# How a split SiLU-and-multiply kernel opens and closes its stores: six first transfers with small packets, 4-row chunks in tile 0, a last tile in two stores

## The chip, the cores and the metric

The kernel runs on one core of a Trainium2 chip. The metric is the device time of one execution in microseconds (us), as the median of several runs. Times inside an execution are taken from its profile and count from the start of the profiled span.

## The reference

```python
batch, seq, dim = (32, 512, 2048)          # x: float32
half_dim = x.shape[-1] // 2
x1, x2 = x[..., :half_dim], x[..., half_dim:]
return (x1 * (1 / (1 + np.exp(-x1))) * x2).astype(np.float32)
```

134.2 MB are read and 67.1 MB written; the arithmetic is one SiLU and one multiply per output element.

## The kernel before

The 16,384 rows are worked off in 16 tiles. A tile has 128 partitions with K = 8 rows each, so a load is 8 MiB in runs of 64 KiB per partition and a store 4 MiB in runs of 32 KiB. There are two input buffers and two output buffers. SiLU runs on ScalarE (ACT) and writes the output tile, the multiply on VectorE (DVE). Loads are issued on the sync queue, stores on the queue of ScalarE.

```python
K = 8
KC_EDGE = 2
OPENING = [                                   # first store: partitions, rows
    (slice(0, None, 4), slice(0, 2)),         # 32 partitions, 8 KiB runs
    (slice(0, None, 4), slice(2, None)),      # 32 partitions, 24 KiB
    (slice(2, None, 4), slice(None)),         # 32 partitions, 32 KiB
    (slice(1, None, 2), slice(None)),         # 64 partitions, 32 KiB
]
in_pool = ctx.enter_context(tc.tile_pool(name="in_pool", bufs=2))
out_pool = ctx.enter_context(tc.tile_pool(name="out_pool", bufs=2))
# ... (cut: the views, load(), silu() on ACT, mul() on DVE)
load(0)
load(1)
for i in range(n_tiles):
    # ... (cut)
    if i < n_tiles - 1:
        kc = KC_EDGE if i == 0 else K
        for c in range(0, K, kc):
            silu(ot, xt, c, c + kc)
            mul(ot, xt, c, c + kc)
        for ps, ks in OPENING if i == 0 else [(slice(None), slice(None))]:
            nc.scalar.dma_start(out=ov[ps, ks], in_=ot[ps, ks])
        if i + 2 < n_tiles:
            load(i + 2)
        continue
    # ... (cut: the last tile, four chunks and four stores of 2 rows)
```

The comments beside OPENING are ours.

## Time and profile before

| | before |
|---|---|
| time, median of 4 runs | 470.53 us (470.48 to 470.60) |
| span of the profiled run | 468.5 us |
| DVE, ACT busy | 30%, 24% |
| load queue and store queue, share of 16 DMA engines | 66.4% and 33.2% |

The lines themselves, and how they are read, stand in the prediction.

### The profile page before, as it was taken

The numbers are of one execution on the slowest core, as the hardware profiler recorded it, in microseconds if no ns is written. First come the engines' busy times: TensorE is split into PE (matmuls) and PEld (weight loads), VectorE is DVE, ScalarE is ACT, GpSimd is POOL, SyncE is SP. The second block draws the span as 40 slices with busy tenths as digits, with TensorE's granted clock in tenths as the row PEclk, the third lists the DMA queues.
The fourth block names the chain that finished last, engine by engine and source line by source line (L and its number), as shares of the span: only waits on it lengthen the run. The fifth ranks groups of instructions, "written<-read, shape, count | busy, mean of one in ns | idle before, by whom it ended". The sixth has DMA issues, their size and how long they took to land.

```text
span 468.5 us, 188 instructions
## 1 busy us (share of the span) xinstructions
DVE 139.5 (30%) x22; ACT 114.3 (24%) x23; POOL 0.2 (0%) x4
## 2 busy tenths in 40 slices
DVE  0070613407033070430704207052060510606151
ACT  1142306041060500505005050140601406023060
POOL 0000000000000000000000000000000000000000
DMA  9999999999999999999999999999999999999988
GB/s 431 392 453 380 448 425 425 492 403 403 448 476 420 403 448 425 470 403 428 422 492 403 403 448 487 408 403 448 425 470 403 425 425 492 403 403 448 481 371 357
DMA packets 5121, 201.34 MB, mean 430 GB/s; under 512 B 608, under 2 KB 608, under 8 KB 608
## 3 DMA queue, kind: packets, MB, share of 16 engines
q1 hardware_dynamic: 2304, 134.22, 66.4%
q10 hardware_dynamic: 2816, 67.11, 33.2%
q14 instruction: 1, 0.01, 0.0%
HBM read 134.22 MB, written 67.11 MB: 430 GB/s over the span
## 4 chain that ended last, share of the span: by engine, by line
DMA 72%; DVE 14%; ACT 11%; DVEq 0%; issue 0%; ACTq 0%
DMA xt<-in_x_dram 72%; DVE ot L91 14%; ACT ot L84 11%; DVEq L148 0%; ACTq L84 0%
## 5 line engine op out<-in xcount | busy, mean ns | idle before, releaser
L91 DVE TENSOR_TENSOR ot<-ot,xt 128x8192 f32<-128x8192 f32 (+1 forms) x22 | 139.5, 6362 | 319.6 <-ACT ot L84 319.6
L84 ACT ACTIVATE ot<-xt 128x8192 f32<-128x8192 f32 (+1 forms) x22 | 113.0, 5163 | 340.5 <-DMA xt<-in_x_dram 340.5
L84 ACT ACT_TABLE_LOAD x1 | 1.3, 1283 | 0.8 <-PEq L137 0.8
L137 POOL MEMSET const-bfloat16-1.0<- 128x1 bf16 x1 | 0.1, 101 | 0.0
L137 POOL MEMSET const-uint8-127<- 128x1 uint8 x1 | 0.1, 101 | 0.0
L137 POOL MEMSET const-float32-0.0<- 128x1 f32 x1 | 0.1, 98 | 0.2 <-issue 0.2
L137 POOL MEMSET const-float32-1.0<- 128x1 f32 x1 | 0.1, 98 | 0.0
## 6 DMA issues: line engine op xcount, KB each, us to landing
out_dram<-ot ACTq DMA_DIRECT2D x14, 4096.0 KB, 42.0
out_dram<-ot ACTq DMA_DIRECT2D x5, 1024.0 KB, 8.2
out_dram<-ot ACTq DMA_DIRECT2D x1, 2048.0 KB, 37.0
out_dram<-ot ACTq DMA_DIRECT2D x1, 768.0 KB, 11.7
xt<-in_x_dram SPq DMA_DIRECT2D x16, 42.1
out_dram<-ot ACTq DMA_DIRECT2D x1, 256.0 KB, 10.9
```

What stands on the lines that cost most here:

```text
L84: nc.scalar.activation(out=ot[:, c:ce, :], in_=xt[:, c:ce, :half], func=mybir.ActivationFunctionType.Silu,)
L91: nc.vector.tensor_mul(out=ot[:, c:ce, :], in0=ot[:, c:ce, :], in1=xt[:, c:ce, half:],)
L137: nc = _bacc.Bacc("TRN2", target_bir_lowering=False, num_devices=1)
```

## The change

The diff suggests this intent: smaller packets at the head of the first store, so that the store takes less from the loads behind which it starts; fewer and larger instructions in tile 0; and fewer, larger stores at the end.

```diff
-    KC_EDGE = 2
+    CHUNKS_FIRST = [4, 4]
+    CHUNKS_LAST = [2, 2, 4]
+    KS = 4
     OPENING = [
         (slice(0, None, 4), slice(0, 2)),
-        (slice(0, None, 4), slice(2, None)),
-        (slice(2, None, 4), slice(None)),
+        (slice(0, None, 4), slice(2, 4)),
+        (slice(0, None, 4), slice(4, None)),
+        (slice(2, None, 4), slice(0, 4)),
+        (slice(2, None, 4), slice(4, None)),
         (slice(1, None, 2), slice(None)),
     ]
 ... (cut: the loop over the chunks of tile 0 now takes CHUNKS_FIRST)
-        cuts = list(range(0, K, KC_EDGE))
 ... (cut: four chunks, each stored two steps later)
+        for kc in CHUNKS_LAST:
+            silu(ot, xt, c, c + kc)
+            if issued is None and c >= KS:
+                issued = slice(0, KS)
+                nc.scalar.dma_start(out=ov[:, issued], in_=ot[:, issued])
+            mul(ot, xt, c, c + kc)
+            c += kc
+        nc.scalar.dma_start(out=ov[:, KS:], in_=ot[:, KS:])
```

More of the change, by code (lines that the diff above doesn't have):

```diff
@@ L103 @@
         if i < n_tiles - 1:
-            kc = KC_EDGE if i == 0 else K
-            for c in range(0, K, kc):
+            c = 0
+            chunks = CHUNKS_FIRST if i == 0 else [K]
+            for kc in chunks:
                 silu(ot, xt, c, c + kc)
                 mul(ot, xt, c, c + kc)
+                c += kc
             for ps, ks in OPENING if i == 0 else [(slice(None), slice(None))]:
@@ L113 @@
             continue
-        cuts = list(range(0, K, KC_EDGE))
-        for n, c in enumerate(cuts + [None, None]):
-            if c is not None:
-                silu(ot, xt, c, c + KC_EDGE)
-                mul(ot, xt, c, c + KC_EDGE)
-            if n >= 2:
-                b = cuts[n - 2]
-                nc.scalar.dma_start(out=ov[:, b:b + KC_EDGE, :], in_=ot[:, b:b + KC_EDGE, :])
+        issued = None
+        c = 0
+        for kc in CHUNKS_LAST:
[4 more added lines that the diff above has]
+            mul(ot, xt, c, c + kc)
+            c += kc
+        nc.scalar.dma_start(out=ov[:, KS:], in_=ot[:, KS:])
 _INS = ['x']
```

## The prediction

> **What bounds the kernel now.** I read the page first: busy shares, the slices, the chain.
>
> ```profile
> span 468.5 us, 188 instructions
> DVE 139.5 (30%) x22; ACT 114.3 (24%) x23; POOL 0.2 (0%) x4
> ...
> DMA  9999999999999999999999999999999999999988
> ...
> q1 hardware_dynamic: 2304, 134.22, 66.4%
> q10 hardware_dynamic: 2816, 67.11, 33.2%
> ...
> DMA 72%; DVE 14%; ACT 11%; DVEq 0%; issue 0%; ACTq 0%
> ```
>
> Both compute engines are idle most of the time. The load queue (q1) and the store queue (q10) together fill 99.6% of the 16 DMA engines. The compute in the chain only separates one load from the next; it lies beside other transfers. The single-packet records of the trace say the same more sharply: from the first load packet, 1.0 us into the span, to the last store packet, which ends at 467.1, no engine pauses visibly. So the kernel moves 201.33 MB with no hole, and only about 1.0 us at the start and 1.4 at the end are not transfer. **There is nearly nothing left to win; the question is whether the change opens a hole.**
>
> The durations come from the groups kept apart by shape:
>
> ```profile
> L91 DVE TENSOR_TENSOR ot<-ot,xt 128x8192 f32<-128x8192 f32 x14 | 121.7, 8692 | 280.6 <-ACT ot L84 280.6
> L84 ACT ACTIVATE ot<-xt 128x8192 f32<-128x8192 f32 x14 | 98.4, 7029 | 298.7 <-DMA xt<-in_x_dram 298.7
> L91 DVE TENSOR_TENSOR ot<-ot,xt 128x2048 f32<-128x2048 f32 x8 | 17.8, 2286 | 39.0 <-ACT ot L84 39.0
> L84 ACT ACTIVATE ot<-xt 128x2048 f32<-128x2048 f32 x8 | 14.6, 1897 | 41.8 <-DMA xt<-in_x_dram 41.8
> ```
>
> A whole tile needs 7.03 + 8.69, with 0.03 between them: 15.75 us from data to store. A 4-row chunk (4096 elements per partition), on the straight line through the two sizes, needs 3.6 us of SiLU and 4.4 of multiply.
>
> Then the timeline of the start:
>
> ```profile
> 21.88 5.51 ACT L84 ACTIVATE ot<-xt 128x2048 f32<-128x2048 f32 x3 [19.83 <-DMA xt<-in_x_dram]
> 23.82 8.90 DVE L91 TENSOR_TENSOR ot<-ot,xt 128x2048 f32<-128x2048 f32 x4 [23.82 <-ACT ot L84]
> 26.15 0.55 ACTq L110 DMA_DIRECT2D out_dram<-ot  x1
> 27.30 1.89 ACT L84 ACTIVATE ot<-xt 128x2048 f32<-128x2048 f32 x1
> 32.75 1.78 ACTq L110 DMA_DIRECT2D out_dram<-ot  x3
> 44.34 7.03 ACT L84 ACTIVATE ot<-xt 128x8192 f32<-128x8192 f32 x1 [15.15 <-DMA xt<-in_x_dram]
> ```
>
> Tile 0 lands at 21.9, its first store goes out at 26.15, the other three from 32.75, and load 1 lands at 44.3.
>
> **The turns.** In the packet records each engine alternates: one packet of the store queue, one of the load queue. A load packet is 64 KiB (2.418 us), a store packet 8 KiB (0.309), 24 KiB (0.912) or 32 KiB (1.213); 16 KiB is then some 0.61. Every transfer ends with a 4-byte packet (9 ns), and that takes a turn too. A full load is 8 + 1 turns, a full store 8 + 1 turns, so in steady state they go in step: 8 x (2.418 + 1.213) = 29.05 us per tile.
>
> The first store sets the phase. Today it has (2+1) + (2+1) + (2+1) + (4+1) = 14 turns. Its first packet goes out with packet 5 of load 1, so there are 5 turns of load 1 left (four packets and its end) and 9 of load 2: also 14. In the records the ends of store 0 and of load 2 do fall in the same turn. This tie matters because there are only two output buffers: SiLU of tile 2 needs load 2 **and** the end of store 0.
>
> **What the Trainium skill says.** "DMA: Bandwidth & Descriptors", section "Queues, rings and completion order": an engine goes round-robin between the queues it has work for, a packet at a time. The trace agrees; but here the switch comes after every single run of 64 or 32 KiB. The same page, "Why a DMA increments its semaphore by 16 and not by 1": the number of engines follows from the outer dimension, and each used engine posts its end. The trace agrees: the transfers of 32 partitions appear as 16 packets twice over, and each transfer leaves 16 packets of 4 bytes. "Latency and other measured facts" there gives about 600 ns to the first byte; the trace's first load took 1.0 us from its issue to its first packet.
>
> **The change part by part.**
>
> Tile 0 in chunks of 4 rows: SiLU 21.88 + 3.6, multiply + 4.4, so the first two stores go out at 29.95 instead of 26.15; the second multiply ends at 34.4 instead of 32.7, then four stores and load 2. Load 2 queues behind load 1, so that delay costs nothing. No engine is idle either: load 1 still has packets. Direct cost 0.
>
> When does the first store packet get a turn? Today it was issued at 26.15, missed the boundary at 28.1 and was taken at 30.7. So it lets pass the packet that runs when it arrives and one more. Issued at 29.95, it falls in load packet 5 (30.5 to 32.9, counting 2.418 a packet from 20.83) or just before, lets packet 6 pass, and is taken at **35.35**, with packet 7.
>
> Six transfers: turns (2+1) + (2+1) + (2+1) + (2+1) + (2+1) + (4+1) = **20 instead of 14**. Of these 3 go with load 1 (packets 7, 8, end), 9 with load 2, and 8 with the eight packets of load 3. In time:
> - load 1 ends at 35.35 + 2 x (0.31 + 2.42) = 40.8, about 3 us earlier than now;
> - load 2 ends at 40.8 + 8 x 2.418 + 2 x 0.31 + 4 x 0.61 = 63.2 (now near 70.1);
> - store 0 ends at 63.2 + 7 x 2.418 + 2 x 0.61 + 4 x 1.213 = 86.2.
>
> To that come 0.45 for the last engine, 0.37 from its end packet to the start of the waiting SiLU (both as in the records of now), and about 1 us, because load packets near the first stores took up to 2.7 to 3.1 us: tile 2 starts at **88.0**, not at 71.27, although its data lie there since about 64.
>
> Tile 2 then takes 15.75 us, so load 4 and store 2 are issued at 103.75 and begin at 104.8. Until then the engines have only loads 0 to 3 and stores 0 and 1, and these bytes were through by 99.2 in the kernel before (SiLU of tile 3 started at 100.05, less the 0.82). **So a hole of 5 to 6 us opens once.** Afterwards load 4 and store 2 start together with 9 turns each and are again in step: end at 104.8 + 29.05 = 133.8, SiLU of tile 4 at 134.6 where the timeline has 129.17 now. Shift **+5.4 us**, and no later stage gives it back, as no stage has spare DMA time.
>
> The last tile: its 32 packets of 8 KiB per engine become 16 of 16 KiB; (32 x 0.309) - (16 x 0.61) = 0.1 us less. Its first store goes out 6.5 us after the data (1.9 + 2.3 + 2.3) instead of 4.3. The store before it keeps the engines busy for 8 x 1.213 = 9.7 us from the end of the last load, 8.9 from the start of SiLU, so 2.4 us are left for the way from issue to first packet, where load 0 took 1.0. Expected cost 0. The second half, at 11.8 us, comes before the first half is through (8.9 + 4.9).
>
> Sum: 470.49 + 5.4 - 0.1 = 475.8.
>
> **The rivals.**
> - *Nothing opens.* If the engines hold enough work to bridge tile 2, only the order of bytes moves: 470.4. For it: 99.6% busy. Against it: at the end of store 0 there is left one load packet and store 1, 2.4 + 9.7 = 12.1 us, against 15.75 + 1.0 + 0.8 needed.
> - *One boundary earlier.* The first packet goes with packet 6: store 0 ends 2.4 us earlier and the hole is 3 us: 473.4. One single observation fixes that latency (over 2.0, under 4.6 us after issue; 3.0 would do), so I give this 30%. A boundary later would make it 478, 5%.
> - *The tail goes dry.* If a store needs over 2.4 us to its first packet, 0 to 2 us are added.
> - *A gain from the earlier loads.* Loads 1 and 2 land 3 and 7 us earlier, but the bytes are the same and the engines were never idle: worth nothing.
>
> **Range and chances.** Weights 0.6 for 475.8, 0.3 for 473.4, the rest for 470.4 and 478, and some tenths for the tail: 475.2. Range 472.4 to 477.4. The 2% limits are 461.1 and 479.9. Faster would need a hole that exists nowhere; slower over 2% would need a hole twice as long, or one that recurs.
>
> **What would show it.** SiLU of tile 1 starts near 41.7 to 42.5, of tile 2 near 88 (85.6 in the rival) after a wait for store 0, not for load 2; the load queue's fifth issue near 103.8; DMA share visibly under full between 99 and 105 and nowhere else; SiLU of tile 4 some 5 us later than now, and the same distance to the end. I am wrong if tile 2 starts on its load's landing (the turns are miscounted or the wait is not on the store), or if the hole is there and a second one appears later.

## The result, and the profile after

The changed kernel took 477.59 us (median of 4 runs, 477.23 to 479.61). The ratio to the kernel before is 1.0156, with a 95% interval of 1.0133 to 1.0178. Ratios here are those of fast runs against fast runs of the kernel before in the same rounds; they are not quite the ratios of the medians. The kernel is 7 us slower; the prediction said 475.2, with 477.4 as its upper end.

From the page of the changed kernel: the span, the DMA rows of the 40 slices, and the shares of the chain that ended last.

```profile
span 477.8 us, 184 instructions
...
DMA  9989999959999999999999999999999999999987
GB/s 439 428 370 475 417 417 428 436 189 428 466 422 403 425 466 403 431 472 411 422 433 461 400 442 464 406 431 469 417 406 439 472 395 433 477 406 428 431 381 313
...
DMA out_dram<-ot 62%; DVE ot L95 16%; ACT ot L88 13%; DMA xt<-in_x_dram 5%; ACTq L116 0%; ACTq L88 0%
```

One slice, the ninth (some 96 to 107 us), has only half its DMA time and 189 GB/s; nothing like it was there before. And the chain now runs through the stores (62%), where it ran through the loads before (72%).

The timeline of the changed kernel, tiles 1 to 4, shows how that came about. Its columns are start, duration, engine, line and operation; in the brackets stands how long the engine was idle before, and what ended the wait.

```profile
30.06 6.81 ACTq L116 DMA_DIRECT2D out_dram<-ot  x6
42.09 7.03 ACT L88 ACTIVATE ot<-xt 128x8192 f32<-128x8192 f32 x1 [13.01 <-DMA xt<-in_x_dram]
...
87.66 7.03 ACT L88 ACTIVATE ot<-xt 128x8192 f32<-128x8192 f32 x1 [38.54 <-DMA out_dram<-ot]
94.72 8.69 DVE L95 TENSOR_TENSOR ot<-ot,xt 128x8192 f32<-128x8192 f32 x1 [36.88 <-ACT ot L88]
103.44 0.36 ACTq L116 DMA_DIRECT2D out_dram<-ot  x1
...
136.21 7.03 ACT L88 ACTIVATE ot<-xt 128x8192 f32<-128x8192 f32 x1 [25.28 <-DMA out_dram<-ot]
```

SiLU of tile 2 starts at 87.66, released by a store. In the kernel before it started at 71.27, released by its load; its SiLU of tiles 2 and 4:

```profile
71.27 7.03 ACT L84 ACTIVATE ot<-xt 128x8192 f32<-128x8192 f32 x1 [19.90 <-DMA xt<-in_x_dram]
...
129.17 7.03 ACT L84 ACTIVATE ot<-xt 128x8192 f32<-128x8192 f32 x1 [22.09 <-DMA xt<-in_x_dram]
```

In the changed kernel, the store of tile 2, and with it load 4, goes out at 103.44. SiLU of tile 4 starts at 136.21; before it was 129.17, so 7.0 us are lost by tile 4, which is the whole loss of a usual run. (This profile fell on the slowest of the four runs, 479.61 us; a second one, below, has nothing beyond these 7 us.)

The stretches around the hole, first in the kernel before, then in the changed one. The last two columns are the mean busy share of the DMA engines and GB/s. A packet is booked whole in the stretch in which it starts, so single stretches swing around 1, and a 0.00 by itself may only mean that no packet started there.

```profile
98.00:100.00 2.00, 0.00 (x0) 0.00 (x0) 0.00 (x0) 1.00 0.62 262
100.00:102.00 2.00, 0.00 (x0) 1.95 (x1) 0.00 (x0) 1.00 1.21 524
102.00:104.00 2.00, 0.00 (x0) 2.00 (x1) 0.00 (x0) 1.00 0.83 360
104.00:106.00 2.00, 0.00 (x0) 2.00 (x1) 0.00 (x0) 1.00 0.98 426
```

```profile
98.00:100.00 2.00, 2.00 (x1) 0.00 (x0) 0.00 (x0) 1.00 0.19 82
100.00:102.00 2.00, 2.00 (x1) 0.00 (x0) 0.00 (x0) 1.00 0.00 0
102.00:104.00 2.00, 1.41 (x1) 0.10 (x1) 0.00 (x0) 1.00 0.00 0
104.00:106.00 2.00, 0.00 (x0) 2.00 (x1) 0.00 (x0) 1.00 1.89 524
```

Two empty stretches in a row, while DVE still multiplies tile 2, are a hole; a store packet of 1.2 us or a load packet of 2.4 cannot hide it. The single-packet records of the changed kernel give it exactly (our own listing, first and last of the 16 engines, times of the span):

```
 86.96 ..  87.34   store queue, end packet of store 0
 99.06 ..  99.44   store queue, end packet of store 1
104.39 .. 105.50   load queue, first packet of load 4, 64 KiB, took 3.35 to 4.17 us
```

On the mean of the engines 5.4 us pass without a packet, and the first load packet afterwards takes 3.78 us on the mean, not the 2.418 that every load packet took in steady state before.

### The profile page after: what moved, and what is told of

Read it like the earlier page. It is cut to its first block, busy times and chain, and to the rows that moved or that the text cites. A ratio compares the mean times of both kernels' runs of the same rounds, so it can differ in the third digit from the quotient of the medians.

```text
span 477.8 us, 184 instructions
## 1 busy us (share of the span) xinstructions
DVE 139.4 (29%) x19; ACT 114.0 (24%) x20; POOL 0.2 (0%) x4
## 4 chain that ended last, share of the span: by engine, by line
DMA 66%; DVE 16%; ACT 13%; another core or an unknown queue 4%; ACTq 0%; issue 0%
DMA out_dram<-ot 62%; DVE ot L95 16%; ACT ot L88 13%; DMA xt<-in_x_dram 5%; ACTq L116 0%; ACTq L88 0%
## 5 line engine op out<-in xcount | busy, mean ns | idle before, releaser
L95 DVE TENSOR_TENSOR ot<-ot,xt 128x8192 f32<-128x8192 f32 (+2 forms) x19 | 139.4, 7344 | 330.0 <-ACT ot L88 330.0
L88 ACT ACTIVATE ot<-xt 128x8192 f32<-128x8192 f32 (+2 forms) x19 | 112.7, 5949 | 350.1 <-DMA out_dram<-ot 308.0
```

The lines of the kernel that those rows point to most:

```text
L88: nc.scalar.activation(out=ot[:, c:ce, :], in_=xt[:, c:ce, :half], func=mybir.ActivationFunctionType.Silu,)
L95: nc.vector.tensor_mul(out=ot[:, c:ce, :], in0=ot[:, c:ce, :], in1=xt[:, c:ce, half:],)
```

## The experiments

**The theories.** A: store 0 has 20 turns, ends late, holds back SiLU of tile 2 through the output buffer, and the DMA engines run dry until load 4 comes. B: each further transfer costs a share of its own. C: the coarser last tile costs the time. A fourth was added, D, which is told below. All kernels gave correct results. "Before" in each round was 470.5 to 470.6 us by the median.

### The number of turns: 17, 19, 21

The unit of theory A is a turn: one packet of the store queue against one of the load queue. One turn more or less moves the end of store 0 by one load packet, 2.4 us. The edits change only OPENING of the changed kernel; splitting a transfer adds one end packet, so one turn.

turns17:

```diff
-        (slice(2, None, 4), slice(0, 4)),
-        (slice(2, None, 4), slice(4, None)),
+        (slice(2, None, 4), slice(None)),
```

> The changed kernel with its fourth and fifth transfer joined (even rows 2 mod 4 whole, 32 KiB packets): 17 turns instead of 20, all else as changed. Theory A (the end of store 0 holds back SiLU of tile 2, and a hole opens where that end comes more than about 5 turns into load 3): store 0 ends 3 load packets earlier than in the changed kernel, SiLU of tile 2 starts near 80.4 us instead of 87.7, its store and load 4 go out near 96, before the engines run dry near 99: no hole, about 470.5 to 471. Theory B (each further transfer costs its share, 7 us over six turns): 474. Theory C (the later and coarser last tile costs the time): 477.

turns19:

```diff
-        (slice(0, None, 4), slice(4, None)),
-        (slice(2, None, 4), slice(0, 4)),
-        (slice(2, None, 4), slice(4, None)),
+        (slice(0, None, 8), slice(4, None)),
+        (slice(4, None, 8), slice(4, None)),
+        (slice(2, None, 8), slice(None)),
+        (slice(6, None, 8), slice(None)),
```

> As turns17, but two of its transfers of 32 partitions are each split into two of 16 partitions: 19 turns. Theory A: store 0 ends one load packet (2.4 us) earlier than in the changed kernel, SiLU of tile 2 near 85.2, the hole near 2.9 us instead of 5.3; with the same slow restart of some 1.7 us, about 475. Theory B: 476.4. Theory C: 477.

turns21:

```diff
-        (slice(1, None, 2), slice(None)),
+        (slice(1, None, 4), slice(None)),
+        (slice(3, None, 4), slice(None)),
```

> The changed kernel with its last transfer (odd partitions) split into two of 32 partitions: 21 turns. Theory A: store 0 ends one load packet later, SiLU of tile 2 near 90.1, the hole near 7.7 us, about 479.9. Theory B: 478.7. Theory C: 477.5.

Measured, with the hole and the first load packet behind it from the packet records (means of the 16 engines):

| | time, median | ratio, 95% interval | hole | first packet over 2.418 | sum |
|---|---|---|---|---|---|
| turns19 | 475.44 | 1.0109 (1.0093 to 1.0125) | 3.1 | 1.3 | 4.4 |
| changed kernel, 20 turns | 477.59 | 1.0156 (1.0133 to 1.0178) | 5.4 | 1.4 | 6.8 |
| turns21 | 480.04 | 1.0211 (1.0189 to 1.0234) | 8.1 | 1.3 | 9.5 |

The losses against the kernel before are 4.9, 7.1 and 9.5 us, and the sums account for nearly all of them. One turn is worth 2.2 and 2.5 us by the medians, as theory A says (2.4); B expected 1.2. In turns21 SiLU of tile 2 starts at 90.34, as expected. The restart costs the same 1.3 to 1.4 us whatever the hole's length. (The sums are rounded from unrounded terms. The profile of the changed kernel is that of its slowest run; its second profile, next section, gives 6.8 again.)

turns17 gave 471.04, 472.93 and 473.16 us in its three fast runs (ratio 1.0053, 1.0033 to 1.0073), and 484.9 and 486.1 in two runs that count as slow because they lie over 1.5% above the fastest; the granted clock is 1.00 in all of them. The fast runs speak against C (477) but do not decide between A (470.5 to 471) and B (474): one has A's value, the other two lie nearer to B's. The scatter is a finding that A did not expect. Its profile fell into a slow run, so no time is read from it here; what it shows of the packets is told under theory D.

### The changed kernel again, for a second profile

> The changed kernel once more, unchanged, for a second profile and three more times: 477.2 to 477.9 in most runs, with a hole of 5.0 to 5.5 us, a first load packet after it of 3.3 to 4.2 us, and ends of the last load on the 16 engines about 1 us apart. The profile seen so far (479.6) had two engines 3.4 us behind; if that is what set it apart, a run near 477.4 does not have it.

No edit. Measured: 477.31 us (477.24 to 477.35), ratio 1.0143 (1.0128 to 1.0158). SiLU of tile 2 started at 87.79, load 4 was issued at 103.57; the hole was 5.5 us, the first load packet behind it took 3.73 on the mean, SiLU of tile 4 started at 136.13. The ends of the last load lay 1.3 us apart on the 16 engines; in the first profile of the changed kernel (479.61) they lay 3.4 apart. So the usual loss is 7 us, and the first profile has some 2 us more that belong to that run: besides the first packets of load 4, 17 load packets between 150 and 174 us took up to 3.24 us, and the ends of a load went from 1.0 us apart at load 4 to 3.3 at load 6.

### The last tile alone, and taken back

tail_only is the kernel before with only the last tile changed; tail_back is the changed kernel with the last tile of before.

```diff
 # tail_only, against the kernel before
-        for n, c in enumerate(cuts + [None, None]):
 ... (cut: its four stores)
+        for kc in CHUNKS_LAST:
 ... (cut: the changed last tile as above; tail_back is the reverse, on the changed kernel)
```

> The kernel before with the last tile of the changed kernel alone. Theory A: the first half goes out before the previous store is through (6.5 us after the data, 8.9 us of store left), so the end does not move: 470.3 to 470.6. Theory C (the tail goes dry): 471.5 or more.

> The changed kernel with the last tile of the kernel before (four stores of 2 rows). Theory A: the hole is at the start, so 477 to 477.6; but as the engines are out of step at the end, finer pieces may give back the about 1.5 us for which most engines stood idle at the last tile, if those engines set the end: then 476. Theory C: near 471.

Measured: tail_only 470.56 us, ratio 1.0001 (0.9986 to 1.0016); tail_back 477.44, ratio 1.0148 (1.0133 to 1.0163). The last tile is worth nothing in either direction; theory C falls. The 1.5 us hoped for in tail_back did not come.

### SiLU of tile 2 without the output buffer

early_silu2 leaves store 0 with its 20 turns, but takes SiLU of tile 2 out of the wait:

```diff
+                if i == 2:
+                    silu(xt, xt, c, c + kc)          # in place, in the input tile
+                    nc.vector.tensor_mul(out=ot[:, c:c + kc, :], in0=xt[:, c:c + kc, :half], in1=xt[:, c:c + kc, half:])
 ... (cut: silu() is told to write only the first half of its target's columns; the other tiles stay as they were)
```

> The changed kernel with all its transfers, but SiLU of tile 2 writes into the input tile, so that it need not wait for store 0; only the multiply of tile 2 does. Theory A: the multiply of tile 2 starts near 87.7, load 4 and store 2 go out near 96.4, before the engines run dry near 99: no hole, about 470.5 to 471, although store 0 has its 20 turns and ends as late as before. Theories B and C: as the changed kernel, 477.5.

Measured: 473.24 us in one run, and 484.14, 485.84 and 487.42 in three that count as slow; there is no ratio. The profile is of the fast run. Its timeline and two of its stretches:

```profile
65.20 7.03 ACT L88 ACTIVATE xt<-xt 128x8192 f32<-128x8192 f32 x1 [15.77 <-DMA xt<-in_x_dram]
88.10 8.69 DVE L113 TENSOR_TENSOR ot<-xt 128x8192 f32<-128x8192 f32 x1 [29.94 <-DMA out_dram<-ot]
96.82 0.36 ACTq L120 DMA_DIRECT2D out_dram<-ot  x1
```

```profile
100.00:102.00 2.00, 0.00 (x0) 1.84 (x1) 0.00 (x0) 1.00 0.49 213
102.00:104.00 2.00, 0.00 (x0) 2.00 (x1) 0.00 (x0) 1.00 1.25 541
```

The mechanics came as expected: the multiply starts when store 0 ends, at 88.10; the next store goes out at 96.82; and the empty stretches are gone. The time is not settled by one run, and the slow ones are not explained here. As a test of the time it is inconclusive; as a test of what opens the hole it agrees with A.

### Each half of the opening alone

six_only is the kernel before with the six transfers of the changed one (the OPENING lines of the diff above, nothing else). chunk_only is the kernel before with

```diff
-            kc = KC_EDGE if i == 0 else K
+            kc = 4 if i == 0 else K
```

> The kernel before with the six transfers alone (tile 0 stays in chunks of 2 rows, the last tile too). Theory A: the first packet goes out with packet 5 of load 1 as before, 20 turns end 6 turns into load 3, two load packets earlier than in the changed kernel: SiLU of tile 2 near 82.8, load 4 near 98.6, first packet 99.5, a hole of half a microsecond at most: 470.5 to 472. Theory B (transfers cost by number): 477.

> The kernel before with tile 0 in chunks of 4 rows alone (four transfers). Theory A: the first packet goes out with packet 7 of load 1, 14 turns end 2 turns into load 3; SiLU of tile 2 starts some 3 to 6 us after its load landed, but the engines keep work until far past load 4: no hole, 470.5. A theory that the later first store alone costs its delay (3.8 us) expects 474.

Measured: six_only 472.94 us, ratio 1.0050 (1.0033 to 1.0067). That is 0.9 us above the range of theory A; theory B, which expected 477, falls. The first packet of load 4 came 0.75 us after the end of store 1 and took 3.63 us on the mean, 1.2 too much: together 2.0 us, where the median lost 2.5. So even a hole of under a microsecond brings nearly the whole restart. (The profile is of the slowest run, 474.85 us; the other three took 472.8 to 473.0.)

chunk_only 480.14 us, ratio 1.0205 (1.0189 to 1.0221). **Here theory A failed outright**: it expected 470.5. There is no hole in this kernel. One long stretch of the middle of the run, the kernel before first, then chunk_only:

```profile
120.00:440.00 320.00, 95.61 (x11) 77.32 (x11) 0.00 (x0) 1.00 1.00 433
```

```profile
120.00:440.00 320.00, 89.76 (x12) 77.32 (x11) 0.00 (x0) 1.00 1.00 427
```

The engines are as busy as before (1.00), but move 427 instead of 433 GB/s: the packets themselves take longer. In the records, 293 of the 1536 packets of loads 4 to 15 took over 0.1 us more than 2.418, 6.2 us per engine in sum; before, not one did. And the ends of one load on the 16 engines drift apart, from 0.6 us at load 2 to 5.5 at the last load, where the kernel before keeps 0.45 throughout. The halves of the opening do not add up: alone they lose 2.5 and 9.7 us, together 7.

### What chunk_only has and the kernel before has not

Theory D: a second cost arises when store 0 ends in a **later turn** than load 2 (the offset). With 14 turns that begin with packet 7 of load 1 instead of packet 5, chunk_only ends store 0 two turns after load 2; the kernel before ends them in the same turn. The next three kernels set that offset through the opening alone, though its transfers differ in more than that: late2 without any change of chunks, tie12 with the chunks of the changed kernel but no offset, early1 with an offset in the other direction.

```diff
 # late2, against the kernel before: 16 turns
-        (slice(0, None, 4), slice(0, 2)),
+        (slice(0, None, 8), slice(0, 2)),
+        (slice(4, None, 8), slice(0, 2)),
         (slice(0, None, 4), slice(2, None)),
-        (slice(2, None, 4), slice(None)),
+        (slice(2, None, 8), slice(None)),
+        (slice(6, None, 8), slice(None)),
```

> The kernel before, with its first and its third transfer of 32 partitions each split into two of 16: 16 turns, taken up with packet 5 of load 1 as before, so that store 0 ends two turns after load 2, as in chunk_only, but without a later or coarser chunk. Theory D: slow as chunk_only, 478 to 481, with the load packets partly above 2.418 us and the ends of one load on the 16 engines some 3 us apart. If the chunks of 4 rows cost: 470.5.

```diff
 # tie12, against the changed kernel: 12 turns in place of its six transfers
+        (slice(0, 16), slice(0, 4)),
+        (slice(0, 16), slice(4, None)),
+        (slice(16, None), slice(None)),
```

> The changed kernel (4-row chunks, its last tile) with a first store of three transfers on contiguous partitions: 1+1, 1+1 and 7+1 packets, 12 turns. Taken up with packet 7 of load 1, 3 + 9 turns are left to the end of load 2, so store 0 ends in the same turn as load 2, as in the kernel before. Theory D (what costs is first the hole, and besides it the 16 engines falling out of step, which comes when store 0 ends in another turn than load 2): 470.5 to 471.5. A theory that the 4-row chunks of tile 0 cost by themselves (chunk_only took 480.1): about 477 to 480.

```diff
 # early1, against the kernel before: 13 turns in place of its four transfers
+        (slice(0, 32), slice(0, 2)),
+        (slice(0, 32), slice(2, None)),
+        (slice(32, None), slice(None)),
```

> The kernel before with a first store of 3 + 3 + 7 = 13 turns on contiguous partitions: store 0 ends one turn before load 2. SiLU of tile 2 waits for its load alone. Theory D in its wide form (any offset puts the engines out of step): above 472. In its narrow form (only a store that ends after the load does): 470.5.

| | offset of store 0 against load 2 | time, median | ratio, 95% interval | load packets over 2.418 by 0.1 us, loads 4 to 15 |
|---|---|---|---|---|
| chunk_only | 2 turns late | 480.14 | 1.0205 (1.0189 to 1.0221) | 293 of 1536 |
| late2 | 2 turns late | 479.74 | 1.0191 (1.0172 to 1.0210) | 267 of 1536 |
| tie12 | none | 471.50 | 1.0018 (1.0001 to 1.0035) | 0 of 1536 |
| early1 | 1 turn early | 472.49 | 1.0041 (1.0026 to 1.0056) | 0 of 1536 |

The same long stretch of the run, late2 first, then tie12:

```profile
120.00:440.00 320.00, 90.62 (x12) 77.32 (x11) 0.00 (x0) 1.00 1.00 426
```

```profile
120.00:440.00 320.00, 95.61 (x11) 77.32 (x11) 0.00 (x0) 1.00 1.00 433
```

So it is not the 4-row chunk: late2 loses the same 9 us without the chunks, and tie12 keeps the chunks and the last tile of the changed kernel and loses 1 us. tie12 is also the plainest proof for the whole change: with the opening alone replaced, 6 of its 7 us are gone. By its time alone, early1 met the wide form of theory D (any offset costs: above 472) and missed the narrow one (470.5). Its packets speak against the wide form all the same: its load packets are all at full speed, and its 2 us, like the 1 us of tie12, are there by load 2 and do not grow. Some of early1's first 32 KiB store packets took up to 2.09 us instead of 1.21; in tie12 it was load packets of up to 3.16 us near the first stores. Both kernels use contiguous partitions; whether that matters was not tested.

Two simpler readings fall as well. Engines out of step with each other are not enough: early1 and tie12 have the ends of each load 2.3 and 2.8 us apart from then on, and no slow packet. A SiLU that waits for a store is not enough: that is so in tile after tile of the changed kernel too. What late2 and chunk_only have and the others have not is an offset that lasts: there the store ends 3.6 to 3.9 us (two turns are one packet of each queue, 1.21 + 2.42) after the load of the same SiLU in nearly every tile, and slow packets come all through the run, 24 to 50 in every 50 us from 50 us on in chunk_only. In the changed kernel only stores 0 and 1 end after their loads.

That goes together with the slow packets in these two kernels; that it causes them is not shown, and one profile speaks against the offset as the only cause. In the slow run of turns17 load 4 and store 2, and all later pairs, end in the same turn, yet 441 of the 1536 packets of loads 4 to 15 are slow. The 17 slow packets in the first profile of the changed kernel came without an offset too. Whether chunk_only and late2 are kernels in which every run is like the slow runs of turns17 was not tested; a run counts as slow only against the fastest of its own kernel.

What slows a load packet was not found: the profile shows the longer packet, not its cause. This stays open. In the changed kernel load 4 and store 2 start together behind the hole, and in the records their ends fall in the same turn again; it does not lose time this way in a usual run. In its second profile only 16 packets of loads 4 to 15 are slow, which are the 16 first ones behind the hole, and it moves 434 GB/s from 120 to 440 us.

No version beat the kernel before; its engines have no hole to close.

## Why the prediction was wrong

The mechanism and nearly every step were right; one term was left out, and the range was pulled away from the right case.

- **Bound by DMA, nothing to win.** Right as far as tried: no kernel of the twelve was faster.
- **The first packet with packet 7 of load 1.** Predicted 35.35, measured 35.55. The rival of one boundary earlier did not happen in either profile of the changed kernel.
- **20 turns.** Load 1 ends at 41.0 (40.8 predicted), load 2 at 63.9 (63.2), store 0 at 87.0 (86.2, before the 1 us that the prediction then allows for longer packets), each on the first of the 16 engines. SiLU of tile 2 at 87.66 (88.0), after a wait for the store.
- **The hole.** Predicted from 99.2 to 104.8, measured 5.4 us on the mean, between 99.2 and 104.6.
- **The step that failed** is "load 4 and store 2 start together with 9 turns each and are again in step: end at 104.8 + 29.05 = 133.8, SiLU of tile 4 at 134.6". It gave the packets after the hole their steady 2.418 us at once. The first load packet after it took 3.78 on the mean (3.35 to 4.17), and SiLU of tile 4 came at 136.21. (The 16 ends of load 4 also lay 1.0 us apart and not 0.45, which adds some 0.5.) The term of 1.3 to 1.4 us was missing in the sum: 470.49 + 5.4 + 1.4 - 0.1 = 477.2, against 477.2 to 477.9 in seven of the eight runs. The trace of before had a hint that was not used: the first packets of load 0, also started on idle engines, took 2.7 to 3.4 us.
- **The range.** The steps summed to 475.8, but the weights drew the figure to 475.2 and the upper end to 477.4, mainly for the rival at 473.4. The measured 477.59 lies 0.2 above that end.
- **The last tile.** Expected cost 0 and gain 0.1 us; tail_only and tail_back show no difference of either sign. Its first store went out 6.5 us after SiLU's start, as predicted.
- **"No later stage gives it back".** Right: the shift is 7.0 us at tile 4 and 7.0 at the end of the second profile (475.5 against 468.5).
- **What the prediction did not ask** is whether a late store 0 has a price without a hole. The same reasoning, applied to the 4-row chunks alone, said 470.5 and was off by almost 10 us. In the changed kernel loads and stores are back in step behind the hole, as the prediction said, and this cost stays away; the prediction did not know that being out of step could cost by itself, so in this it was lucky.

## What to carry to other kernels

When two DMA queues share the engines packet by packet, count turns, end packets included: how many packets a transfer is cut into decides when it ends, and through a double buffer that decides when the next load can be issued. Where the engines are full, compare the work still queued with the time from the release of the buffer to the next transfer's first packet; if it falls short, add the hole and also a restart on idle engines (here 1.2 to 1.4 us). And look whether a store ends later than the load for which the same SiLU waits, tile after tile: the two kernels here in which it did lost 9 us, for a reason that stays open.

## What the Trainium skill lacked or had wrong

- "DMA: Bandwidth & Descriptors", section "Queues, rings and completion order", has an engine drain a packet of typically about 9 to 17 descriptors of one queue before it switches. For the long runs of this kernel that count does not hold: it switched after every single run of 8 to 64 KiB, and the 4-byte end packet took a turn of its own; one turn was worth 2.2 and 2.5 us. (Elsewhere the page prefers packets of at most 4096 B, which would leave such runs alone in a packet.)
- The same page, "Latency and other measured facts", gives about 600 ns to the first byte; the first load here took 1.0 us from its issue to its first packet. The section has no price for a restart: load 4 began about 1.2 us after its issue on the mean of the engines, and its first 64 KiB packet took 3.6 to 3.8 us on the mean instead of 2.418, after holes of 0.75 to 8 us alike.
- No page has it that load packets can run slower while the DMA engines stay fully busy, as in the two kernels whose stores end two turns after the loads: 427 and 426 instead of 433 GB/s, 9 us. The cause is open.
- "DMA: Bandwidth & Descriptors", section "Where 436 GB/s comes from", has the HBM side, about 358 GB/s, bind transfers between HBM and SBUF. That does not hold for this one core: the kernel before moved 433 GB/s from 120 to 440 us, loads and stores together, close to the fabric ceiling of 435 GB/s in the same section.
